# Rests of the down weights from a negated copy and a transfer that adds, in the second gated network of a hybrid decoder trunk

## The chip, the cores and the metric

The kernel runs on one core of a Trainium2 chip. The core has TensorE (PE, matmuls; its weight loads are shown apart as PEld), VectorE (DVE), ScalarE (ACT), GpSimd (POOL) and SyncE (SP), which work side by side and wait for each other by semaphores. 16 DMA engines move data between memory (HBM) and the core's buffer (SBUF); the orders for them stand in queues, here mostly SP's, and for some transfers POOL's. The metric is the device time of one execution in microseconds (us).

## What is computed

Two residual layers over 512 tokens of width 1024: first an S5 mixer, then FoX attention, each followed by a gated network with a causal convolution of width 3. Each part is modulated by shift, scale and gate from a conditioning vector. The part that matters here:

```python
def conv_ffn(h, w_up, conv_w, conv_b, w_down):
    up = h @ w_up
    a, b = jnp.split(up, 2, axis=-1)
    S = a.shape[1]
    ap = jnp.pad(a, ((0, 0), (CONV_W - 1, 0), (0, 0)))
    a_conv = conv_b
    for i in range(CONV_W):
        a_conv = a_conv + ap[:, i:i + S] * conv_w[i]
    return (jax.nn.silu(a_conv) * b) @ w_down

h = h + gate * conv_ffn(hn, ffn_w_up[i], ffn_conv_w[i], ffn_conv_b[i], ffn_w_down[i])
```

Here `w_up` is 1024 x 5632 and `w_down` 2816 x 1024, all in float32, and the tokens lie along the columns of the tiles.

## The kernel before

**Two parts of each number.** A float32 matrix product is done as three matmuls in a rounded format (fp32r): a number is split into its rounded value `hi` and the rest `lo`, and hi·hi + hi·lo + lo·hi is added up in PSUM (`mms`, line 294; in the second way of multiplying below, line 550). A weight tile comes from memory by a load on SP's queue into a buffer `raw` (line 186, three buffers that all weights share in turn), then `put_parts` makes the parts: ACT copies `raw` into `w_hi`, which rounds it (line 277), and DVE subtracts `raw` - `w_hi` into `w_lo` (line 278). Five buffers each of `w_hi` and `w_lo` are shared by these weights in turn. `split` (line 269) is the load and the two parts of one block.

**The gated network** (`ffn`). Its 22 blocks of 128 hidden channels are cut into groups; in the second network these are groups of 6, 5, 6 and 5. The first four blocks use plain products. From then on `quarters` computes both up products of a block (a and b) with seven half-width products in place of eight, which need sums and differences of weights: DVE makes them (line 518, `sums`), ACT and DVE split them, and the products go into two PSUM tiles named `mmp` and two named `aux`. Three of the products are copied out of an `mmp` tile by ACT (`nm_h`, line 557) before PE adds the next product to that tile. A fourth copy is from `aux`. Then follow the convolution and the gate (lines 600, 602, 605 and 612) and the split of the hidden block into `ghi` and `glo` (lines 277 and 278).

**Down products.** While group q is computed, the down products of group q - 1 are worked off: after each hidden block one or two of the eight output tiles (`down` through `product`, `weights` and `split`). One tile takes the down weights of one group for 128 output channels: 6 (or 5) blocks of 128 x 128, so one tile of 128 x 768 (or 640), and 18 (or 15) matmuls of 512 columns (line 294); the third of these is the first that reads `w_lo`. The result is added to the residual by DVE (line 362). The down products of the last group come at the end, behind all blocks.

**What sets the order.** The code names the work of a block in turn; the recording layer then orders the instructions of each engine by when it reckons that each can start. Once built, each engine works its list off in that order, and each waits by semaphores for what it reads and for buffers to come free.

Of the kernel before, what the change touches and what calls it, by code (L numbers as in the profile page):

```python
# [11 lines left out]
AF = mybir.ActivationFunctionType  # L12
ALU = mybir.AluOpType
# [45 lines left out]
def fill(pool, n):  # L59

    pool.tile([P, n // 4], F32, name="fill", bufs=1)
# [5 lines left out]
def part_of(pool, shape, name, tag, bufs, aside=0):  # L67

    _, n, w = shape
    t = pool.tile([P, ROOM if bufs == WB else n * w + P], F32R, name=name, tag=tag, bufs=bufs)  # L70
    return t[:, aside:aside + n * w].rearrange("p (n w) -> p n w", w=w)


class Trunk:
# [6 lines left out]
    def __init__(self, tc, io, ctx):  # L81
        self.tc, self.nc, self.io, self.ctx = tc, tc.nc, io, ctx
        nc = self.nc
        pool = lambda name, bufs, **k: ctx.enter_context(tc.tile_pool(name=name, bufs=bufs, **k))
        self.const = pool("const", 1)
        self.act = pool("act", 1)
        self.wpool = pool("wpool", 3)
        self.tmp = pool("tmp", 2)
        self.small = pool("small", 2)
        self.dram = pool("dram", 1, space=DRAM)  # L90
        self.mm = pool("mm", 4, space=PSUM)
        self.aux = pool("aux", 4, space=PSUM)
        self.bg = []
        self.acc = None
        self.pending = None
        self.normed, self.evac, self.copied, self.squared = [], [], [], []
        self.sums = {}

        self.room = None
        self.one = self.const.tile([P, 1], F32, name="one")  # L100
        nc.vector.memset(self.one, 1.0)
        self.sc = self.const.tile([P, KT], F32, name="sc")
        self.scd = self.dram.tile([KT, P], F32, name="scd")

        self.sel = self.const.tile([P, 6], F32, name="sel")
        nc.gpsimd.memset(self.sel, 0.0)
        for q in range(4):
            for c in (q, 4 + q % 2):
                nc.gpsimd.memset(self.sel[32 * q:32 * q + 1, c:c + 1], 1.0)
        self.par = [self.const.tile([P, 24], F32, name=f"par{i}") for i in range(4)]  # L110
        self.ga = [self.const.tile([P, KT], F32, name=f"ga{i}") for i in range(4)]
        fill(self.const, 1728)
        fill(self.small, 1440 - 1024)
# [155 lines left out]
    def split(self, src, shape, pool=None, bufs=WB, aside=0):  # L269

        hi, lo = (part_of(pool or self.wpool, shape, n, n, bufs, aside) for n in ("w_hi", "w_lo"))
        self.put_parts(hi, lo, self.raw(shape, src))
        return hi, lo

    def put_parts(self, hi, lo, src):
# [307 lines left out]
    def ffn(self, i, l, x, nxt, ticks=0, plain=None):  # L583

        nc, tc = self.nc, self.tc
        with tc.tile_pool(name=f"ffn{l}", bufs=1, reuse_waits="tile") as pool:
            self.bgpool = pool
            conv = pool.tile([P, 4, FT], F32, name="conv_wb")
            nc.sync.dma_start(conv, self.io["conv"][l])
            fill(pool, 1696)  # L590
            cw, cb = conv[:, :3], conv[:, 3]
            groups = QGROUPS[l] if plain else GROUPS
            first = [sum(groups[:q]) for q in range(len(groups) + 1)]
            keep, g = {}, {}

            def gated(m, ps, cols):
                f = m // 2
                if m % 2 == 0:
                    t = pool.tile([P, S], F32, name="conv", bufs=2 if plain else 3)
                    nc.scalar.activation(t, ps, AF.Identity, bias=cb[:, f:f + 1], scale=cw[:, 2, f:f + 1])  # L600
                    for d in (1, 2):
                        c = nc.vector.scalar_tensor_tensor(
                            t[:, d:], ps[:, :S - d], cw[:, 2 - d, f:f + 1], t[:, d:], op0=ALU.mult, op1=ALU.add
                        )
                    nc.scalar.activation(t, t, AF.Silu)
                    keep[f] = t
                    if plain and f >= groups[0]:
                        self.evac = [c.ins]
                        self.tick(ticks)
                    return  # L610
                t = keep.pop(f)
                nc.vector.tensor_tensor(t, t, ps, ALU.mult)
                q = sum(f >= n for n in first[1:])
                j = f - first[q]
                if not j:
                    tag = f"{q % 2}" if plain else ""
                    g[q] = [pool.tile([P, groups[q], S], F32R, name=n, tag=n + tag) for n in ("ghi", "glo")]
                hi, lo = g[q]
                self.put_parts(hi[:, j, :], lo[:, j, :], t)

            after, y = nxt
            up = lambda fs, **k: self.product(
                self.io["w_up"][l], range(2 * fs[0], 2 * fs[-1] + 2), KT, x, gated,
                ticks=0 if plain else ticks, **k
            )
            last = len(groups) - 1
            down = lambda q, ms, **k: self.product(
                self.io["w_down"][l][:, :, first[q]:first[q + 1], :], ms, groups[q], g[q],
                self.add_residual(i, q == last), after=after, ticks=0 if plain else ticks, **k
            )  # L630
            todo = []
            for q, n in enumerate(groups):
                fs = range(first[q], first[q + 1])
                if not plain:
                    up(fs, head=0 if q else 3)
                    if q < last:
                        down(q, range(KT))
                    continue
                for j, f in enumerate(fs):
                    if f == 0:  # L640
                        up([0, 1], head=3)
                        todo.append(self.forms_x(pool, x))
                    elif f in plain:
                        if f > 1:
                            up([f])
                        for _ in range(4):
                            if todo and next(todo[0], True):
                                todo.pop()
                    else:
                        while todo:  # L650
                            if next(todo[0], True):
                                todo.pop()
                        self.quarters(pool, l, f, x, gated)
                    if q:
                        self.room = "rawd" if ticks else None
                        down(q - 1, range(j * KT // n, (j + 1) * KT // n))
                        self.room = None
                        self.tick(ticks)
            down(last, range(KT), tail=TAIL if plain else 2, tail_pool=(pool, 4))
        return y  # L660
# [985 lines left out]
```

## Time and profile before

| | |
|---|---|
| time, median of 3 runs (lowest to highest) | 1214.67 us (1213.35 to 1220.85) |
| profiled execution: its own time | 1217.02 us |
| profiled execution: span from the first to the last instruction | 1215.2 us |
| mean granted clock of PE over the span | 0.995 |
| loads from memory over the span | 175.57 MB read, 6.92 MB written |
| transfers of down weights on SP's queue into `raw`: KB each, us to landing | 384.0, 3.5 and 320.0, 3.1 |

Rows of the profile name the engine, the line of the kernel's file, the operation and `out<-in` by the names of the tiles; `xN` counts instructions. In a row of a group the number behind the bar is the busy time and the mean of one in ns, and behind the second bar stands how long the engine stood idle just before them, and for whom. In a timeline a row begins with the start in us and the duration, and ends with the idle time before it in brackets. In the chain of waits a row is a piece of the chain that ended last: start, length, engine and line. Windows give the busy time of each engine in a stretch.

The second gated network fills about 861 to 1205 us of the span; the part of it from 920 to 1168 us is where the down products of the first three groups are prepared and worked off.

### The profile page before, as it was taken

How to read it: one execution, taken by the hardware profiler on the slowest of the kernel's cores; microseconds unless marked ns; L12 is line 12 of the kernel's file. 1: busy time of each engine (PE TensorE's matmuls, PEld its weight loads, DVE VectorE, ACT ScalarE, POOL GpSimd, SP SyncE). 2: the span in 40 equal slices, each digit the busy share in tenths (PEclk: the TensorE clock that was granted, in tenths of full speed). 3: DMA queues.
4: the chain of work that ended last, by engine and by line, in shares of the span. 5: the costliest groups of instructions: out<-in, count | busy, mean ns of one | idle time of the engine just before them, and what ended most of it. 6: DMA issues, size and time to landing. Idle time of an engine off the chain costs nothing.

```text
span 1215.2 us, 20334 instructions
## 1 busy us (share of the span) xinstructions
PE 1180.3 (97%) x7793; PEld 1015.4 (84%) x7793; DVE 1007.6 (83%) x1872; ACT 609.8 (50%) x1156; POOL 83.9 (7%) x145
## 2 busy tenths in 40 slices
PE   7999999999999999999999999999999999999997
PEld 2566688898989899889899777878989999999987
DVE  7999977789899988898687578875899887888965
ACT  3644555336445454455443565654466554555543
POOL 0000000100000000000000333430000000000000
PEclk9999999999999999999999999999999999999999
DMA  9778786622455544553445543432213332333331
GB/s 348 243 250 261 233 294 220 210 77 70 136 179 164 189 155 148 169 168 106 126 153 180 172 153 130 148 108 88 89 53 113 112 119 90 103 104 109 109 100 70
DMA packets 74512, 183.81 MB, mean 151 GB/s; under 512 B 23231, under 2 KB 25631, under 8 KB 73391
## 3 DMA queue, kind: packets, MB, share of 16 engines
q1 hardware_dynamic: 68367, 161.02, 40.5%
q0 software_dynamic: 5760, 20.97, 5.4%
q8 instruction: 61, 1.00, 0.3%
q10 hardware_dynamic: 288, 0.52, 0.1%
q14 instruction: 36, 0.29, 0.1%
HBM read 175.57 MB, written 6.92 MB: 150 GB/s over the span
## 4 chain that ended last, share of the span: by engine, by line
PE 56%; issue 26%; DVE 8%; DMA 5%; ACT 2%; POOL 2%; SPq 0%; POOLq 0%; DVEq 0%; ACTq 0%
PE mmp L294 24%; PE mmp L550 11%; PE aux L550 4%; PE mmp L1366 3%; PE mmp L1174 2%; DVE w_lo L278 2%; PE mmp L1203 2%; POOL ada_raw L233 1%; PE aux L1505 1%; DMA ada_raw<-in_ada_t 1%; PE aux L1065 1%; PE mmp L1114 1%; PE aux L1057 1%; PE aux L978 1%; DMA yt<-s_yd 1%
## 5 line engine op out<-in xcount | busy, mean ns | idle before, releaser
L278 DVE TENSOR_TENSOR w_lo<-raw,w_hi 128x1024 fp32r<-128x1024 f32 (+4 forms) x173 | 183.3, 1064 | 37.6 <-ACT w_hi L277 31.8
L277 ACT ACTIVATE w_hi<-raw 128x1024 fp32r<-128x1024 f32 (+4 forms) x173 | 154.8, 904 | 105.4 <-PE mmp L294 48.6
L294 PE MATMUL mmp<-ghi,w_hi 128*128 128x512 f32 (+1 forms) x392 | 145.5, 371 | 0.0
L294 PE MATMUL mmp<-ghi,w_lo 128*128 128x512 f32 (+1 forms) x392 | 144.7, 369 | 0.7 <-DVE w_lo L278 0.6
L294 PE MATMUL mmp<-glo,w_hi 128*128 128x512 f32 (+1 forms) x392 | 145.1, 370 | 0.0
L294 PE MATMUL mmp<-a_hi,w_hi 128*128 128x512 f32 (+1 forms) x376 | 138.4, 371 | 1.5 <-ACT a_hi L433 1.5
L294 PE MATMUL mmp<-a_hi,w_lo 128*128 128x512 f32 (+1 forms) x376 | 136.2, 363 | 0.2 <-DVE w_lo L278 0.2
L294 PE MATMUL mmp<-a_lo,w_hi 128*128 128x512 f32 (+1 forms) x376 | 135.7, 362 | 0.0
L550 PE MATMUL mmp<-w_hi 128*128 128x256 f32 x396 | 109.7, 277 | 2.7 <-ACT nm_h L557 2.3
L550 PE MATMUL mmp<-w_hi,w_lo 128*128 128x256 f32 x396 | 109.5, 277 | 0.7 <-DVE w_lo L278 0.7
L550 PE MATMUL mmp<-w_lo,w_hi 128*128 128x256 f32 x396 | 109.4, 276 | 0.0
L557 ACT ACTIVATE nm_h<-mmp 128x256 f32<-128x256 f32 x99 | 37.2, 381 | 107.3 <-PE mmp L550 107.3
L278 DVE TENSOR_TENSOR w_lo<-sums,w_hi 128x1024 fp32r<-128x1024 f32 x74 | 90.0, 1219 | 0.0
L277 ACT ACTIVATE w_hi<-sums 128x1024 fp32r<-128x1024 f32 x74 | 77.0, 1055 | 23.7 <-DVE sums L518 21.7
L294 PEld LDWEIGHTS mmp<-ghi,w_lo 128*128 128x128 f32 x392 | 74.7, 190 | 13.8 <-DVE w_lo L278 1.5
L294 PEld LDWEIGHTS mmp<-ghi,w_hi 128*128 128x128 f32 x392 | 74.7, 191 | 11.5 <-ACT w_hi L277 0.2
L294 PEld LDWEIGHTS mmp<-glo,w_hi 128*128 128x128 f32 x392 | 74.8, 191 | 11.1
L294 PEld LDWEIGHTS mmp<-a_hi,w_hi 128*128 128x128 f32 x376 | 70.2, 188 | 13.8 <-issue 2.6
L294 PEld LDWEIGHTS mmp<-a_hi,w_lo 128*128 128x128 f32 x376 | 70.6, 188 | 12.2 <-DVE w_lo L278 1.2
L294 PEld LDWEIGHTS mmp<-a_lo,w_hi 128*128 128x128 f32 x376 | 70.7, 188 | 9.7
L362 DVE SCALAR_TENSOR_TENSOR h<-mmp,par,h 128x512 f32<-128x512 f32 (+1 forms) x100 | 68.0, 681 | 12.1 <-PE mmp L294 11.9
L550 PEld LDWEIGHTS mmp<-w_hi 128*128 128x128 f32 x396 | 74.3, 188 | 3.2 <-ACT nm_h L557 2.5
(319 smaller groups left out, 3077.7 us busy)
## 6 DMA issues: line engine op xcount, KB each, us to landing
raw<-in_w_up SPq DMA_DIRECT2D x88, 512.0 KB, 3.3
raw<-in_ada_w SPq DMA_DIRECT2D x40, 512.0 KB, 5.6
ada_raw<-in_ada_t POOLq DMA_DIRECT2D x40, 512.0 KB, 3.9
nf<-nfd SPq DMA_DIRECT2D x8, 1152.0 KB, 6.5
raw<-in_fox_qk SPq DMA_DIRECT2D x16, 512.0 KB, 3.7
raw<-in_w_down SPq DMA_DIRECT2D x24, 320.0 KB, 3.1
rawd<-in_w_down SPq DMA_DIRECT2D x24, 256.0 KB, 3.3
raw<-in_w_down SPq DMA_DIRECT2D x16, 384.0 KB, 3.5
```

Of the source, the lines that this page charges most:

```text
L233: (nc.gpsimd if late else nc.sync).dma_start(ws[n], src)
L277: nc.scalar.activation(hi, src, AF.Copy)
L278: return nc.vector.tensor_tensor(lo, src, hi.bitcast(F32), ALU.subtract)
L294: self.last_mm = self.nc.tensor.matmul(o, wt, xt[:, cols], start=(k == 0 and n == 0), stop=(k == nk - 1 and n == 2),)
L362: add = self.nc.vector.scalar_tensor_tensor(self.h[:, m, cols], ps, self.par[i][:, 16 + m:17 + m], self.h[:, m, cols], op0=ALU.mult, op1=A ...
L550: self.last_mm = nc.tensor.matmul(o, wt[:, k], xt[:, k], start=(first and k == 0 and n == 0), stop=(k == H - 1 and n == 2), skip_group_che ...
L557: a = nc.scalar.activation(t, o, AF.Copy)
L978: nc.tensor.matmul(ps[:, :, cols], x[:, q, r].rearrange("p c j -> p (c j)"), both[:, :, planes, q, :], start=(r == 0), stop=(r == 1), skip ...
L1057: nc.tensor.matmul(yp[g2][:, k, :], t[:, g].rearrange("p c i -> p (c i)"), u[:, g, :], start=(k == 0), stop=False, skip_group_check=True,)
L1174: nc.tensor.matmul(ps, w[m][:, k, :], x[:, k], start=(k == 0), stop=(k == KT - 1))
L1203: nc.tensor.matmul(gps[m], wt, xt[:, k], start=(k == 0 and part == 0 and xt is yhi), stop=(k == KT - 1 and part == 1))
L1366: self.last_mm = nc.tensor.matmul(ps[q, b][:, :n], xt[:, k, tb], wt, start=(k == 0 and i == 0), stop=(k == KT - 1 and i == 2),)
```

## The change

In the second gated network, for the down weights of its first three groups, the rest is no longer made by DVE. ACT copies the raw weights twice: into `w_hi`, rounded, and with a factor of -1 into `w_lo`, which then holds the negated rounded value. A transfer on POOL's queue then reads the same raw weights from memory again and adds them to what lies in `w_lo`, so that raw - rounded remains. The down weights of the first network, those of the last group, and all up weights are made as before.

```diff
     def split(self, src, shape, pool=None, bufs=WB, aside=0):
 
         hi, lo = (part_of(pool or self.wpool, shape, n, n, bufs, aside) for n in ("w_hi", "w_lo"))
-        self.put_parts(hi, lo, self.raw(shape, src))
+        raw = self.raw(shape, src)
+        if self.adds:
+            self.nc.scalar.activation(lo, raw, AF.Copy, scale=-1.0)
+            self.nc.scalar.activation(hi, raw, AF.Copy)
+            self.nc.gpsimd.dma_start(lo, src, accum_op=ALU.add)
+        else:
+            self.put_parts(hi, lo, raw)
         return hi, lo
...
                     if q:
                         self.room = "rawd" if ticks else None
+                        self.adds = not ticks
                         down(q - 1, range(j * KT // n, (j + 1) * KT // n))
+                        self.adds = False
                         self.room = None
```

`ticks` is 1 in the first network and 0 in the second; `self.adds` is False from the start.

In the built program PE's list and SP's list hold the same instructions in the same order. The other three move. On ACT, around the first 768-wide down weight of the third group (in the trace of before, the place from 1092 to 1099 us), before:

```order
L277 ACTIVATE w_hi<-raw 128x512
L557 ACTIVATE nm_h<-aux 128x256
L277 ACTIVATE w_hi<-sums 128x1024
L605 ACTIVATE conv<-conv 128x512
L277 ACTIVATE ghi<-conv 128x512
L277 ACTIVATE w_hi<-sums 128x1024
L277 ACTIVATE w_hi<-raw 128x768
L557 ACTIVATE nm_h<-mmp 128x256 x3
```

And now at the same place; the lines of the file are seven higher behind the edit, line 284 is the copy of `put_parts`, 275 and 276 are the two of the new path:

```order
L564 ACTIVATE nm_h<-aux 128x256
L284 ACTIVATE w_hi<-raw 128x512
L284 ACTIVATE w_hi<-sums 128x1024
L612 ACTIVATE conv<-conv 128x512
L276 ACTIVATE w_hi<-raw 128x768
L284 ACTIVATE ghi<-conv 128x512
L275 ACTIVATE w_lo<-raw 128x768
L564 ACTIVATE nm_h<-mmp 128x256 x3
```

The down weight's first copy now stands ahead of the copy of the hidden block and its second copy right behind it; both are still ahead of the three copies out of PSUM.

On DVE, the turn around the same place before, from the sums of a block to its convolution:

```order
L278 TENSOR_TENSOR w_lo<-raw,w_hi 128x768
L518 TENSOR_TENSOR sums<-raw 128x512
L518 TENSOR_TENSOR nm_t<-aux,nm_h 128x256
L518 TENSOR_TENSOR sums<-sums,raw 128x512
L518 TENSOR_TENSOR sums<-raw 128x512
L518 TENSOR_TENSOR sums<-raw,sums 128x512
L278 TENSOR_TENSOR w_lo<-raw,w_hi 128x1024
```

And now:

```order
L525 TENSOR_TENSOR sums<-raw 128x512 x2
L525 TENSOR_TENSOR sums<-sums,raw 128x512
L525 TENSOR_TENSOR sums<-raw,sums 128x512
L525 TENSOR_TENSOR nm_t<-aux,nm_h 128x256
L285 TENSOR_TENSOR w_lo<-raw,w_hi 128x1024
```

The subtraction for the down weight is gone, and the four sums of a block stand in a row ahead of the addition for the output. On POOL's list the 24 transfers stand behind all else that POOL does:

```order
L1505 TENSOR_SCALAR s_8611<-s_8611,sm 128x512 x2
L277 DMA w_lo<-in_w_down 128x768 x8
L277 DMA w_lo<-in_w_down 128x640 x8
L277 DMA w_lo<-in_w_down 128x768 x8
L1647 UNCONDITIONAL_BRANCH
```

Before, the branch followed the row of line 1505 (1496 then) at once.

More of the change, by code (lines that the diff above doesn't have):

```diff
@@ L655, in ffn @@
                         self.room = "rawd" if ticks else None
+                        self.adds = not ticks
                         down(q - 1, range(j * KT // n, (j + 1) * KT // n))
+                        self.adds = False
                         self.room = None
```

## The prediction

> **What bounds the kernel now.** I read the page's table of engines first, then the stage of the second gated network by windows, then the chain of waits there, then the groups of DVE and ACT of that stage, and last single rows around the down weights. The page has TensorE busy for nearly the whole span, and the stage in which the change works (920 to 1168 us, where the down weights of the first three groups are prepared) leaves no gap in it at all.
>
> ```profile
> PE 1180.3 (97%) x7793; PEld 1015.4 (84%) x7793; DVE 1007.6 (83%) x1872; ACT 609.8 (50%) x1156; POOL 83.9 (7%) x145
> 920.00:1168.00 248.00, 248.00 (x1809) 233.11 (x1809) 210.99 (x318) 133.33 (x212) 0.00 (x0) 1.00 0.35 109
> ```
>
> The second line gives, in order, the busy time of PE, its weight loads, DVE, ACT and POOL in the 248 us, the granted clock and the share of the DMA engines. A busy PE need not be a PE at its peak, so I checked its pace in the chain that ended last. One turn of the loop is there from 1095.36 on: seven quarter products of 12 matmuls each, then one down tile of 18.
>
> ```profile
> 1095.36 2.74 PE mmp L550 x24
> 1098.11 1.36 PE aux L550 x12
> 1099.47 2.85 PE mmp L550 x24
> 1102.31 1.36 PE aux L550 x12
> 1103.67 1.36 PE mmp L550 x12
> 1105.03 4.10 PE mmp L294 x18
> ```
>
> The chain is PE after PE with no other engine in it. A 256-column matmul passes every 0.113 us (1.36 / 12) and a 512-column one every 0.228 us (4.10 / 18), and the pieces start where the last one ended. The only irregular piece is the third, 2.85 us for 24 matmuls where the first took 2.74: about 0.1 us. That is all that better preparation of weights could win in this turn; the granted clock is 1.00 already.
>
> **The change part by part.** *What DVE and ACT do.* These are the groups of the two kinds of down weights in the stage; the 640-wide ones are ten here because two belong to the last group, which the change leaves alone.
>
> ```profile
> L278 DVE TENSOR_TENSOR w_lo<-raw,w_hi 128x768 fp32r<-128x768 f32 x16 | 14.9, 949 | 0.6 <-ACT w_hi L277 0.6
> L278 DVE TENSOR_TENSOR w_lo<-raw,w_hi 128x640 fp32r<-128x640 f32 x10 | 8.0, 819 | 0.7 <-ACT w_hi L277 0.7
> L277 ACT ACTIVATE w_hi<-raw 128x768 fp32r<-128x768 f32 x16 | 13.3, 834 | 4.6 <-PE mmp L294 3.5 <-DMA raw<-in_w_down 1.2
> L277 ACT ACTIVATE w_hi<-raw 128x640 fp32r<-128x640 f32 x10 | 7.3, 732 | 3.0 <-PE mmp L294 1.5 <-PE aux L550 0.9 <-PE mmp L550 0.6
> L518 DVE TENSOR_TENSOR sums<-raw 128x512 f32<-128x512 f32 x32 | 21.2, 687 | 23.4 <-DMA raw<-in_w_up 23.4
> ```
>
> DVE loses 16 x 0.949 + 8 x 0.819 = 21.7 us of its 211.0. ACT gains as many copies, 16 x 0.834 + 8 x 0.732 = 19.2 us on 133.3, which makes 152.5 of 248 (61%). Neither is on the chain, so both count nothing toward the end as long as PE finds its weights. DVE's gain goes into its own idle time. The last row shows where it idles: 23.4 us for raw up weights, whose three buffers come free only once DVE has read them. A down weight's buffer is now given back by ACT's second copy and no longer by DVE's late subtraction, so those loads can start sooner; SP issues the same transfers in the same order.
>
> *The new transfer.* 24 transfers are issued on POOL's queue, which has no work in this stage, so nothing but the next transfer stands behind a waiting one. PE waits for the result. No accumulating transfer is in the trace; the nearest rows are the 40 plain loads that POOL issues for the adaLN weights, 512 KB each, in the first gated network.
>
> ```profile
> L233 POOL DMA_DIRECT2D ada_raw<-in_ada_t x40: 527/530/743, 158.4 to 555.2; - x40
> DMA to landing us min/median/max: 3.6/3.9/6.8
> q0 software_dynamic: 5760, 20.97, 5.4%
> ```
>
> Issuing takes 0.53 us, so 24 of them are 12.7 us of an empty queue. From issue to landing it is 3.9 us. The packets took 5.4% of 1215.2 us for 40 loads, 1.64 us each, so 2.26 of the 3.9 us do not depend on size. A down weight has 384 KB (or 320), 1.23 us at that pace. An accumulating transfer must also fetch what lies in the destination. I take twice the bytes, 2.26 + 2.46 = 4.7 us, as an estimate. The low end is the plain price for the smaller size, 3.5 us; the high end is the slowest load seen plus one more such load's packets, 6.8 + 1.64 = 8.4 us. The Trainium skill (Collectives: The Full Stack, section "The bandwidth ceiling: the fold count and why AG ≠ RS ≠ AR") says that a transfer that adds runs at about half the rate of a copy, and that the second source read is the reason, not the addition. No run here shows this yet; by it the landing would also be 4.7 us and the sum the same.
>
> *How much time there is.* For each down weight I take the end of ACT's copy in the trace, add the second copy, and compare with the first matmul that reads the rest, the third of its tile. Two rows show that this one starts 0.3 us after the start of the tile in the chain.
>
> ```profile
> 953.48 8.19 PE mmp L294 x36
> 953.78 0.39 PE L294 MATMUL mmp<-ghi,w_lo 128*128 128x512 f32 x1
> 1105.34 0.39 PE L294 MATMUL mmp<-ghi,w_lo 128*128 128x512 f32 x1
> 946.59 0.83 ACT L277 ACTIVATE w_hi<-raw 128x768 fp32r<-128x768 f32 x1
> 1097.17 1.06 ACT L277 ACTIVATE w_hi<-sums 128x1024 fp32r<-128x1024 f32 x1 [1.89 <-DVE sums L518]
> 1098.14 0.83 ACT L277 ACTIVATE w_hi<-raw 128x768 fp32r<-128x768 f32 x1
> 1098.87 0.64 ACT L557 ACTIVATE nm_h<-mmp 128x256 f32<-128x256 f32 x2
> ```
>
> Copies in a row start 0.73 us apart (1098.14 to 1098.87), so two of them end 0.73 + 0.83 = 1.56 us after the first began. At 1098.14 that is 1099.70, and the rest is read at 1105.34: 5.6 us. At 946.59 it is 948.15 against 953.78: 5.6 us again. These are the two tightest. The next are these, the ACT row first and the tile in the chain behind it:
>
> ```profile
> 1054.33 0.72 ACT L277 ACTIVATE w_hi<-raw 128x640 fp32r<-128x640 f32 x1
> 1062.61 3.42 PE mmp L294 x15
> 930.44 1.36 ACT L277 ACTIVATE w_hi<-raw 128x512 fp32r<-128x512 f32 x2
> 939.83 4.10 PE mmp L294 x18
> 1127.08 0.83 ACT L277 ACTIVATE w_hi<-raw 128x768 fp32r<-128x768 f32 x1
> 1136.41 4.10 PE mmp L294 x18
> 961.79 0.83 ACT L277 ACTIVATE w_hi<-raw 128x768 fp32r<-128x768 f32 x1
> 971.21 4.10 PE mmp L294 x18
> 1077.37 1.25 ACT L277 ACTIVATE w_hi<-raw 128x512 fp32r<-128x512 f32 x2
> 1088.54 6.82 PE mmp L294 x30
> ```
>
> In the same way they leave 7.2, 7.6, 8.1, 8.2 and 9.6 us (a row of "x2" ends with the down weight). One more, the second weight for the tiles from 953.48 on, has 7.4 us, but it lies behind the tight one there, whose wait would cover it. The other 16 have 9.7 us or more. With 4.7 us none is late. With the high end of 8.4 us the waits are 2 x 2.8 + 1.2 + 0.8 + 0.3 + 0.2 = 8.1 us.
>
> *DMA load.* 24 x 2.46 us is 59 us of 248, on top of a share of 0.35, so 0.59. That makes other loads a little later; DVE has the 21.7 us that it was relieved of to take that up.
>
> **Sum.** Removed from the chain: 0.1 us at most. Added: 0, up to 8.1 us at the high end. Against the profiled execution (span 1215.2 us, its own time 1217.02) that is no change. The median of the three runs is 2.35 us below the profiled one, so I count from there: 1214.67 - 0.1, about 1214.5 us.
>
> **The rivals.** *A: the rests land too late.* An addition in the DMA engines might be far slower than two reads; nothing in the trace bounds it. The place is the third matmul of each down tile. With 9 us to landing the waits are 2 x 3.4 + 1.8 + 1.4 + 0.9 + 0.8 = 11.7 us, about 1%: that is the point from which this decides. With 10 us it is 2 x 4.4 + 2.8 + 2.4 + 1.9 + 1.8 + 0.4 = 18.1 us, and a little more from the other 16: 1233 us. For it speaks that the kind is unseen; against it that 9 us would be some 5.5 times the packet time of the plain load, (9 - 2.26) / 1.23.
>
> *B: DVE holds POOL up.* While DVE works without a gap POOL might not get its descriptors written. DVE has runs of 12 us without a gap, from 1088.13 to 1100.36:
>
> ```profile
> 1088.13 0.69 DVE L518 TENSOR_TENSOR sums<-raw 128x512 f32<-128x512 f32 x1 [3.08 <-DMA raw<-in_w_up]
> 1099.41 0.95 DVE L278 TENSOR_TENSOR w_lo<-raw,w_hi 128x768 fp32r<-128x768 f32 x1
> 1101.85 0.69 DVE L518 TENSOR_TENSOR sums<-raw 128x512 f32<-128x512 f32 x1 [1.49 <-DMA raw<-in_w_up]
> 380.00:580.00 200.00, 194.64 (x1296) 176.61 (x1295) 179.25 (x283) 93.38 (x152) 12.17 (x23) 1.00 0.49 158
> ```
>
> Half a run on top of 4.7 us makes 10.7 us, and waits of 2 x 5.1 + 3.5 + 3.1 + 2.6 + 2.5 + 1.1 = 23.0 us: 1238 us. Against it stand the 23 issues of the last row's window, 12.17 us in all, 0.53 us each, beside a DVE that was busy 179.25 of 200 us. The Trainium skill (SBUF — State Buffer, section "🔬 SBUF: two separate sides") warns that a transfer issued from GpSimd sits without descriptors while DVE runs an operation that takes both port pairs; the trace shows none of that in the 40 issues, 0.743 us at the longest.
>
> *C: ACT becomes the bound.* Its copies out of PSUM (nm_h) free the tile that PE adds to next. The row at 1098.87 stands behind a down weight, ends at 1099.5, and the third piece of the chain is the one that is 0.1 us long. If each of the 24 added copies held PE up for its whole 0.7 us, it would be 17 us: 1231 us. Against it: PE returns to such a tile 2.72 us after it was done (two products of 1.36 us), and ACT's copy needs less than 0.4 (0.64 for the two in that row), which leaves some 2.3 us for one or two copies ahead of it; and the 1.89 us that ACT stood before 1097.17 was for DVE, which now has less to do.
>
> *D: faster by over 1%.* That would take 12 us out of a stage whose PE has no gap at full clock; 0.1 us is all I find. 1202 us at best, by a cause that I do not see.
>
> **How the numbers follow.** About 1% is what a measurement of this kernel can tell from no change. The forecast, waits between 0 and 8 us, has 0.81. A, beyond 9 us, has 0.11, since its price is unseen; B 0.02; C with more than 12 us 0.04; D 0.02. So faster 0.02, same 0.81, slower 0.17. The range starts at 1212, a little below the fastest run before (1213.35), holds the high end of the sum (1214.5 + 8.1 = 1222.6) and C's full price (1231), and ends at 1232; outside lie most of A, B and D, some 0.15.
>
> **What would show it.** Right: PE busy for 248 of 248 us in the stage, DVE near 190 us, ACT near 152, and no row in which PE waited for a transfer into w_lo. The time from issue to landing of these transfers decides: near 5 us for the forecast, over 9 us for A; issues far over 0.53 us for B; PE waiting for ACT's nm_h for C. Wrong would be a time over 1227, or PE idle before the third matmul of a down tile.

## The result and the profile after

The changed kernel takes 1222.11 us, median of 19 runs (1216.66 to 1231.98); the kernel before took 1215.49 us in 19 runs beside it (1212.58 to 1220.85). The ratio is 1.0055, with a 95% interval from 1.0036 to 1.0074: about half a per cent slower, small but clear of no change, since with 19 runs each the interval is only 0.2% to either side. The profiled execution took 1221.81 us, its span is 1220.0 us.

First come the page's table of engines and the window of the stage, both of the changed kernel, with the columns of the prediction's first fence:

```profile
PE 1184.2 (97%) x7793; PEld 1017.1 (83%) x7793; DVE 988.0 (81%) x1848; ACT 625.3 (51%) x1180; POOL 103.2 (8%) x169
920.00:1168.00 248.00, 245.35 (x1779) 229.04 (x1778) 189.81 (x291) 147.50 (x233) 20.50 (x24) 1.00 0.52 139
```

DVE lost 21 us in the stage and ACT gained 14 there, with fewer matmuls passed in the same 248 us (1779 for 1809). PE is no longer busy throughout: 2.65 us are missing, at a granted clock of 1.00. What it waited for stands in the view of waits of the changed kernel (who waits, for what: us in all, times, the longest):

```profile
PEld mmp L301 <- DMA w_lo<-in_w_down: 4.4, 4, 2.7
PE mmp L301 <- DMA w_lo<-in_w_down: 2.6, 2, 2.2
```

Before there was no such row. The chain of waits shows what that made of the stage. This is its row at the last of these down tiles in the kernel before (the first is in the prediction):

```profile
1167.78 22.26 PE mmp L294 x100
```

and these are the rows at the first and the last in the changed kernel:

```profile
939.32 1.38 PE mmp L557 x12
940.70 0.03 POOLq L277
...
1172.31 17.70 PE mmp L301 x78
```

A transfer order of POOL's queue now stands in the chain where PE ran on before. From the start of the first down tile to that of the last it was 1167.78 - 939.83 = 227.95 us; it is 1172.31 - 940.70 = 231.61 us now, 3.66 us more. In the timeline of PE the whole of it is found at four tiles, each time at the third matmul (a row is start, duration, what, and in brackets the idle time before it and for whom):

```profile
940.75 0.40 PE L301 MATMUL mmp<-glo,w_hi 128*128 128x512 f32 x1
943.38 0.50 PE L301 MATMUL mmp<-ghi,w_lo 128*128 128x512 f32 x1 [2.24 <-DMA w_lo<-in_w_down]
...
957.66 0.50 PE L301 MATMUL mmp<-ghi,w_lo 128*128 128x512 f32 x1 [0.34 <-DMA w_lo<-in_w_down]
...
1123.00 0.50 PE L301 MATMUL mmp<-ghi,w_lo 128*128 128x512 f32 x1
...
1141.11 0.50 PE L301 MATMUL mmp<-ghi,w_lo 128*128 128x512 f32 x1
```

A 512-column matmul follows the last one after 0.23 us when nothing is in its way. 943.38 comes 2.63 us after 940.75, so 2.40 us late; in the same way the other three are 0.50, 0.13 and 0.25 us late, and the matmul behind each of the four another 0.1. That adds up to 3.7 us.

Last come the transfers, in the groups by tile (min/median/max of the issue in ns) and in the table of DMA of the changed kernel, from 920 us on:

```profile
L277 POOL DMA_DIRECT2D w_lo<-in_w_down x24: 847/855/902, 935.4 to 1166.4; - x24
DMA to landing us min/median/max: 4.9/7.4/9.9
```

```profile
q0 software_dynamic: 3456, 8.91, 20.3%
w_lo<-in_w_down POOLq DMA_DIRECT2D x16, 384.0 KB, 8.0
w_lo<-in_w_down POOLq DMA_DIRECT2D x8, 320.0 KB, 6.4
```

From issue to landing it is 7.4 us in the middle, where the forecast had 4.7, and 8.0 for the wide weights. The packets took 20.3% of the 255 us of this window (920 to 1175) for 24 transfers, 2.16 us each.

### The profile page after: what moved, and what is told of

It reads as the page before. It is cut to its first block, busy times and chain, and to the rows that moved or that the text cites. A ratio compares the mean times of both kernels' runs of the same rounds, so it can differ in the third digit from the quotient of the medians.

```text
span 1220.0 us, 20390 instructions
## 1 busy us (share of the span) xinstructions
PE 1184.2 (97%) x7793; PEld 1017.1 (83%) x7793; DVE 988.0 (81%) x1848; ACT 625.3 (51%) x1180; POOL 103.2 (8%) x169
## 4 chain that ended last, share of the span: by engine, by line
PE 49%; issue 26%; DVE 12%; DMA 8%; ACT 2%; POOL 1%; SPq 0%; POOLq 0%; DVEq 0%; ACTq 0%
PE mmp L301 24%; PE mmp L557 4%; DVE w_lo L285 4%; PE mmp L1375 3%; PE mmp L1183 3%; DMA w_lo<-in_w_down 3%; PE aux L557 2%; PE mmp L1212 2%; DMA rawd<-in_w_down 1%; PE aux L1514 1%; PE aux L1074 1%; PE aux L987 1%; PE mmp L1123 1%; PE aux L1066 1%; DVE ada_raw L248 1%
## 5 line engine op out<-in xcount | busy, mean ns | idle before, releaser
L285 DVE TENSOR_TENSOR w_lo<-raw,w_hi 128x1024 fp32r<-128x1024 f32 (+3 forms) x149 | 161.1, 1084 | 42.8 <-ACT w_hi L284 36.7
L284 ACT ACTIVATE w_hi<-raw 128x1024 fp32r<-128x1024 f32 (+3 forms) x149 | 136.3, 921 | 98.3 <-PE mmp L301 44.8
```

What stands on the lines that cost most here:

```text
L284: nc.scalar.activation(hi, src, AF.Copy)
L285: return nc.vector.tensor_tensor(lo, src, hi.bitcast(F32), ALU.subtract)
```

## The experiments

Three theories were open. Theory 1: the whole loss is PE's wait at a few tiles for rests that land late, and they land late because the transfer adds. Theory 2: the landing is long because each transfer meets loads of SP that ACT's copies have just released. Theory 3: the added copies on ACT, or the added traffic, cost something beside those waits.

### e1_plain: the same transfer without the addition

```diff
-            self.nc.gpsimd.dma_start(lo, src, accum_op=ALU.add)
+            self.nc.gpsimd.dma_start(lo, src)
```

> Leaves out the addition: the transfer on POOL's queue loads the raw weights into w_lo instead of adding them, so the rests are wrong by the rounded value; all else, the places of the 24 transfers and the buffers, is as in the changed kernel. Theory 1 (the loss is PE's wait at a few tiles for rests that take 7.4 us to land, and the addition makes them slow): issue 0.53 instead of 0.855 us, landing near 4 us, no PE wait for w_lo, time within 0.2% of before. Theory 2 (the landing is long because each transfer meets the load that SP issues 0.3 us ahead of it): landing 6 us or more here too, and a wait at the first tile stays. Theory 3 (the loss is the added copies and traffic, not the landing): time as in the changed kernel, ratio 1.004 to 1.007.

Measured: 1215.94 us, ratio 1.0000 (0.9983 to 1.0018). The window and the transfers of this run:

```profile
920.00:1168.00 248.00, 248.00 (x1810) 232.88 (x1809) 192.26 (x294) 150.15 (x238) 12.75 (x24) 1.00 0.44 144
```

```profile
L277 POOL DMA_DIRECT2D w_lo<-in_w_down x24: 527/527/604, 935.6 to 1161.1; - x24
DMA to landing us min/median/max: 3.5/4.5/6.4
```

```profile
q0 software_dynamic: 3456, 8.91, 10.6%
w_lo<-in_w_down POOLq DMA_DIRECT2D x16, 384.0 KB, 4.9
w_lo<-in_w_down POOLq DMA_DIRECT2D x8, 320.0 KB, 4.1
```

PE's gaps are gone, with all copies, all transfers and their order as in the changed kernel. The instruction lists of all five engines are the same in both kernels. So the addition is what makes the rests late. It costs 0.33 us at the issue (0.855 for 0.527), 1.03 us of packets (2.16 for 10.6% x 255 / 24 = 1.13) and 2.9 us to the landing (7.4 for 4.5): more than its packet time explains.

The packet records of the traces show where the rest lies. Four of the 384 KB transfers overlap no other of their queue. In the changed kernel the first packet of these starts 2.4 us after the issue, the packets are spread over 3.8 us, and the landing comes 0.3 us after the last (medians). In e1_plain it is 2.1, 1.5 and 0.3 us. Here the addition lengthens the stretch from the first to the last packet, and hardly the time ahead of it.

### e2_lo_first: the negated copy first on ACT

```diff
-            self.nc.scalar.activation(lo, raw, AF.Copy, scale=-1.0)
-            self.nc.scalar.activation(hi, raw, AF.Copy)
+            neg = self.nc.scalar.activation(lo, raw, AF.Copy, scale=-1.0)
+            with self.behind(neg.ins):
+                self.nc.scalar.activation(hi, raw, AF.Copy)
```

> As the changed kernel, but ACT makes the negated copy first and the rounded one after it, so that the transfer is issued ahead of the raw buffer's release and of the load on SP's queue that follows from it. Theory 1: the transfer starts 0.8 to 2.4 us sooner; the wait of 2.4 us at the first down tile goes and the other three (0.5, 0.13, 0.25 us) too, so the time comes within 0.2% of before. Theory 2 (meeting SP's load): the landing itself also falls by 1 to 2 us. Theory 3 (added copies and traffic): no change from the changed kernel.

Measured: 1231.55 us, ratio 1.0140 (1.0108 to 1.0172), a miss. The forced order did not bring the negated copy forward; it kept its old place among ACT's work and pushed the rounded copy behind it. The waits of this run (the line of `product` is 302 here):

```profile
PEld mmp L302 <- DMA w_lo<-in_w_down: 4.7, 2, 3.6
PE mmp L558 <- ACT nm_h L565: 9.0, 5, 3.0
DVE sums L526 <- DMA raw<-in_w_up: 50.7, 14, 6.3
```

The rests still come late at two tiles, and now PE also waits for ACT's copies out of PSUM, behind a DVE that waits longer for raw loads (50.7 us; 38.0 in the changed kernel, 23.4 before). This is the prediction's rival C, brought about by the experiment, not by the change. As a test of slack it failed. It does say something of theory 2: the transfers land after 6.8 us in the middle, 0.6 less than in the changed kernel, where that theory asked for 1 to 2 less.

### e3_group1: only the 640-wide weights by transfer

```diff
-                        self.adds = not ticks
+                        self.adds = not ticks and q == 2
```

> The transfer only for the second group (eight 640-wide down weights); the first and third groups are made by DVE as before. Theory 1: none of the four tiles that waited is in this group, so no PE wait for w_lo and a ratio to before of 1.000 +- 0.002. Theory 3 (each added copy and transfer costs a little): a third of the loss stays, about 1.002.

Measured: 1217.1 us, ratio 1.0007 (0.9990 to 1.0024). The window, and the landing of the eight transfers that are left:

```profile
920.00:1168.00 248.00, 248.00 (x1803) 232.81 (x1802) 205.11 (x310) 137.98 (x220) 6.87 (x8) 1.00 0.41 118
```

```profile
DMA to landing us min/median/max: 5.1/6.6/7.9
```

The eight transfers add as slowly as in the changed kernel (6.6 against 6.4 us), and cost nothing, since their tiles have the time. What counts is the landing against the slack of the tile, not the landing.

### e4_copy_only: the second copy without the transfer

```diff
             self.nc.scalar.activation(lo, raw, AF.Copy, scale=-1.0)
-            self.nc.scalar.activation(hi, raw, AF.Copy)
-            self.nc.gpsimd.dma_start(lo, src, accum_op=ALU.add)
+            self.put_parts(hi, lo, raw)
```

> As before the change, but with ACT's second copy (negated, into w_lo) ahead of the rounded copy and of DVE's subtraction, which overwrites it; no transfer on POOL's queue. Nothing of the result is left out. Theory 1: no PE wait comes of it, ratio to before 1.000 +- 0.002. Theory 3 in the form that ACT's 19 us of copies delay its copies out of PSUM: PE waits for nm_h and a ratio of 1.004 or more.

Measured: 1217.29 us, ratio 1.0007 (0.9994 to 1.0020); the window of the stage has ACT at 148.89 us and PE at 247.62. What PE lacks there is one wait for a copy out of PSUM:

```profile
1099.62 0.39 PE L556 MATMUL mmp<-w_hi 128*128 128x256 f32 x1 [0.38 <-ACT nm_h L563]
```

So the 24 copies on ACT can hold PE up, but by 0.4 us in this profile and by nothing clear of noise in the medians. As the cause of the loss theory 3 falls for the copies by this run, and for the traffic by e1_plain.

### e6_skip4: four steps (six tiles) made as before

```diff
-                        self.adds = not ticks
+                        self.adds = not ticks and (q, j) not in ((1, 0), (1, 1), (3, 1), (3, 2))
```

> As the changed kernel, but the down weights of four steps (six tiles: the first, second and third of the first group, the second to fourth of the third group), where the trace of the changed kernel has all its waits, are made by DVE as before; 18 of the 24 transfers stay. Theory 1 (all of the loss is these waits): no PE wait for a transfer, ratio to before 1.000 +- 0.002. Theory 3 (each transfer costs something): three quarters of the loss stay, ratio 1.003 to 1.005.

Measured: 1216.42 us, ratio 1.0003 (0.9985 to 1.0021). 18 of the 24 transfers stay, and the loss is gone. In its profile the landing of the 18 is as long as ever, and PE still waits for a rest once, 0.59 us:

```profile
DMA to landing us min/median/max: 5.5/7.6/9.7
```

```profile
999.55 0.50 PE L301 MATMUL mmp<-ghi,w_lo 128*128 128x512 f32 x1 [0.59 <-DMA w_lo<-in_w_down]
```

It also waits once for a copy of ACT out of PSUM (`nm_h`), 0.47 us at 992.62. The loss lies in those few tiles; this is what theory 1 says.

### e8_twice: the rest added twice

```diff
             self.nc.gpsimd.dma_start(lo, src, accum_op=ALU.add)
+            self.nc.gpsimd.dma_start(lo, src, accum_op=ALU.add)
```

> As the changed kernel, but the raw weights are added twice, the second transfer waiting for the first, so that the rests are wrong by the raw value and land at about 15 us. Theory 1 by the slack that each tile has: about half of the tiles wait, 3 to 7 us each, some 50 to 80 us in all, ratio 1.04 to 1.07. If PE's waits were not what costs the time, the ratio would stay under 1.02.

Measured: 1269.79 us, ratio 1.0448 (1.0412 to 1.0484). The same mechanism in large: the second transfer waits for the first, and PE waits for rests at 14 places in the row of its weight loads, over the whole span:

```profile
PEld mmp L302 <- DMA w_lo<-in_w_down: 42.7, 14, 6.8
```

The 42.7 us are the idle time of the weight loads, which is a little longer than what PE loses. In the timeline of PE the third matmul is late at 13 tiles, by 39.0 us in all, and the steps behind them are some 14 us longer than usual, nearly all of it because PE ran at half its pace behind the longest waits; the last section shows that. Together these are about 53 us, and the medians differ by 54.2.

### e5_probe: the transfers by themselves

The kernel before, with 18 transfers in a chain on POOL's queue at the start of the second gated network, each of which waits for the last: plain, plain into a rounded tile, and adding; first of 384 KB, then of 192.

```diff
+        for n in (6, 3):
+            for _ in range(3):
+                nc.gpsimd.dma_start(t[:, :n].bitcast(F32), src[:, :n])
+            for _ in range(3):
+                nc.gpsimd.dma_start(t[:, :n], src[:, :n])
+            for _ in range(3):
+                nc.gpsimd.dma_start(t[:, :n], src[:, :n], accum_op=ALU.add)
```

> The kernel before, with a chain of transfers beside it that nothing uses: at the start of the second gated network POOL issues, each waiting for the one ahead of it, three plain loads of 384 KB as float32, three plain loads of 384 KB into the rounded format, three adding ones of 384 KB, and the same nine with 192 KB. Nothing of the result is left out. If the addition by itself makes the landing long: adding transfers of 384 KB take 6 us or more here too, some 3 us above the plain ones, with 0.85 us to issue. If meeting SP's released load makes it long: about 5 us when few loads are about. If the part that depends on size rules, 192 KB lands 1 us or more sooner than 384 KB when it adds; if a fixed part rules, less than 0.5 us.

Measured: the landings by line in this run, in the order above, from 860 to 907 us (384 KB) and from 907 to 946 us (192 KB):

```profile
L670 POOL DMA_DIRECT2D probe<-in_w_down x3: 536/553/589, 865.5 to 872.9; - x3
DMA to landing us min/median/max: 3.4/3.4/4.9
...
L672 POOL DMA_DIRECT2D probe<-in_w_down x3: 527/527/536, 878.0 to 885.5; - x3
DMA to landing us min/median/max: 3.4/3.5/3.5
...
L674 POOL DMA_DIRECT2D probe<-in_w_down x3: 858/866/897, 889.3 to 902.6; - x3
DMA to landing us min/median/max: 4.9/6.1/6.3
...
L674 POOL DMA_DIRECT2D probe<-in_w_down x3: 856/862/884, 930.7 to 941.1; - x3
DMA to landing us min/median/max: 3.7/4.7/5.1
```

The type costs nothing (3.5 for 3.4 us). The addition costs 2.6 us at 384 KB; at 192 KB an adding transfer takes 4.7 us where the two plain lines had 3.6 and 3.2. So of the 3.1 us that the addition costs in the kernel (8.0 for 4.9), it costs 2.6 in the chain too, and there it costs more for the larger size. The split seen in e1_plain does not hold in the chain: two of the three adding 384 KB transfers start their first packet only 3.2 and 3.5 us after the issue, the plain ones after 1.2 to 1.4.

In the kernel's own place a plain transfer of 384 KB took 4.9 us and an adding one 8.0, that is 1.4 and 1.9 us more than in the chain. That much is left for theory 2; that SP's loads are what makes it was not tried by itself. The traces point to something nearer: most of the 24 transfers come in pairs, for two tiles behind the same hidden block, and overlap. In the first profile of the changed kernel a 384 KB transfer that overlaps no other of its queue lands after 6.8 us, the first of a pair after 7.8, the second after 8.9 (medians of 4, 6 and 6); in e1_plain it is 4.1, 4.7 and 5.7.

### e7_halves: each rest by two transfers

```diff
+            n = shape[1] // 2
-            self.nc.gpsimd.dma_start(lo, src, accum_op=ALU.add)
+            self.nc.gpsimd.dma_start(lo[:, :n], src[:, :n], accum_op=ALU.add)
+            self.nc.gpsimd.dma_start(lo[:, n:], src[:, n:], accum_op=ALU.add)
```

> As the changed kernel, but each rest is added by two transfers, one for the first half of the blocks and one for the second, issued one behind the other. Theory 1 with a landing that grows with size: the first half, which the third matmul of a tile needs, lands at 5 to 6 us, the waits shrink to under 1 us in all, ratio about 1.001. With a landing that is mostly fixed: both halves land at 7 us or more, and the loss stays as in the changed kernel or grows, ratio 1.005 or more.

Measured: 1217.52 us, ratio 1.0013 (0.9997 to 1.0029). The third matmul needs only the first half, and that lands earlier, but only by 0.8 us in the middle (6.6 for 7.4; the first half by its line, the second by its own):

```profile
L278 POOL DMA_DIRECT2D w_lo<-in_w_down x24: 855/855/1166, 933.5 to 1160.9; - x24
DMA to landing us min/median/max: 3.5/6.6/8.9
...
L279 POOL DMA_DIRECT2D w_lo<-in_w_down x24: 1014/1194/1505, 934.1 to 1161.4; - x24
DMA to landing us min/median/max: 4.4/7.4/9.3
```

PE waits at one tile only, the first, 1.28 us. That wins back most of the loss, and still does not beat the kernel before.

### e9_again and e10_again: the changed kernel profiled twice more

The first profile's 3.7 us of waits leave open what makes the 6.6 us between the medians, so the unaltered kernel was profiled again.

> The changed kernel unaltered, profiled once more. The first profile's stage grew by 3.7 us of waits for rests, while the medians differ by 6.6 us. Theory 1 (the whole loss is waits for late rests, and their size varies from execution to execution with the landing): another profile has waits for w_lo of another size, 2 to 12 us in sum from 936 us on, at the same tiles (the first one among them) and possibly at one or two more, and the time from the start of the first down tile to the start of the last one grows over the 227.95 us of before by that sum within 0.3 us. Rival (a fixed cost beside the waits): the waits are again 3.7 us within 0.5 us, and what is missing to 6.6 us lies outside these tiles or in gaps that wait for something else.

> The same kernel a third time, on the same chip: with three profiles the spread of the waits can be seen. Theory 1: the times of the three profiled executions stand in the same order as their sums of waits for rests, and differ by about as much. Rival: they do not follow the waits.

Measured: 1219.30 and 1222.66 us, beside one run of the kernel before at 1212.31. The chain of waits at the first and at the last down tile, of e9_again:

```profile
939.04 0.03 POOLq L277
...
1169.85 28.61 PE mmp L301 x156
```

and of e10_again:

```profile
938.50 0.03 POOLq L277
...
1173.24 26.79 PE mmp L301 x140
```

From the one to the other it is 1169.85 - 939.04 = 230.81 us in e9_again and 1173.24 - 938.50 = 234.74 us in e10_again, 2.86 and 6.79 us more than before. The late steps of PE add up to 3.0 and 6.8 us. The first tile is 0.68 us late in the one, 3.42 in the other, and 2.40 in the first profile; its matmul is due 5.6 us after the issue in all three, and the transfer landed after 6.3, 9.0 and 8.0 us. The second tile is late in all three as well. In the third group the tiles change: the first one of it, on time in the first profile, is late in both of these, in e9_again like this:

```profile
1107.30 0.50 PE L301 MATMUL mmp<-ghi,w_lo 128*128 128x512 f32 x1 [0.45 <-DMA w_lo<-in_w_down]
```

The tile that was late at 1123.00 is late again in e10_again alone (0.07 us), and the one at 1141.11 in neither. Of all 72 transfers of the three profiles, 11 land later after their issue than the matmul is due, and at the third matmul of these 11 tiles, and of no other, PE is late, by that difference within 0.1 us.

So the waits vary from execution to execution because the landing does, and with 2.9, 3.7 and 6.8 us the three times stand in the order of their waits (1219.30, 1221.81, 1222.66). They do not differ by just as much: the first tile starts between 938.50 and 940.70 us, so the stages before differ by up to 2.2 us as well. The three waits have a mean of 4.4 us, which is the low edge of the interval of the difference (0.36% to 0.74%, 4.4 to 9.0 us). For the other 2 us up to the difference of the medians three profiles are too few, and no cause of their own was seen; that the loss as a whole hangs on the late rests is shown by e1_plain and e6_skip4, whose medians are those of before.

## Why the prediction was wrong

The forecast was no change, 1214.5 us; the kernel is 0.55% slower, beyond what the runs are uncertain by, though inside the given range and within 1%. The prediction held that about 1% is what can be told from no change; these runs can tell half of that.

- **The step that failed: the landing of the new transfer.** The prediction took "twice the bytes, 2.26 + 2.46 = 4.7 us". Measured are 7.4 us (8.0 for the wide weights, up to 9.9). The doubled packet time was right in kind and near in size: 2.16 us, 1.9 times the 1.13 us of the plain transfer in e1_plain, where the estimate was 2.46. The Trainium skill (Collectives: The Full Stack, section "The bandwidth ceiling: the fold count and why AG ≠ RS ≠ AR") has a collective that adds (ReduceScatter) run at half the rate of one that copies (AllGather), because the addition reads two sources; the packet times here agree with that. What failed was the 2.26 us beside the packets, taken as fixed: in the changed kernel 7.4 - 2.16 = 5.2 us lie there, and in e1_plain 4.5 - 1.13 = 3.4. About one us of the miss already belongs to the place, where a plain transfer takes 4.5 us and two transfers of the queue overlap for most tiles, which the prediction did not price; the larger part is the addition's, as e1_plain and e5_probe show. By the packet records of the 384 KB transfers that no other overlaps, the time ahead of the first packet and behind the last stayed in the kernel nearly what it is for a plain one; the time between the two is what grew, from 1.5 to 3.8 us, more than the packet time of such a transfer did.
- **The sum at the high end was the right one.** With 8.4 us the prediction had waits of 8.1 us and 1222.6 us; with 8.0 us its table gives 2 x 2.4 + 0.4 = 5.2 us (the 640-wide weight with 7.2 us is in time, since its kind lands after 6.4). The three profiles have 2.9, 3.7 and 6.8. The mechanism was that of rival A, well short of its 9 us. The error lay in taking 4.7 us and not the high end as the forecast for a kind of transfer of which the trace had none.
- **The slack of single tiles was off.** The first tile had 7.6 us in the prediction, from the ACT list of before. On the new list a copy out of PSUM and an activation stand between the two copies, in the timeline of ACT of the changed kernel:

```profile
931.82 0.83 ACT L276 ACTIVATE w_hi<-raw 128x768 fp32r<-128x768 f32 x1
932.62 0.38 ACT L564 ACTIVATE nm_h<-mmp 128x256 f32<-128x256 f32 x1
933.67 0.63 ACT L612 ACTIVATE conv<-conv 128x512 f32<-128x512 f32 x1 [0.67 <-DVE conv L609]
934.21 0.83 ACT L275 ACTIVATE w_lo<-raw 128x768 fp32r<-128x768 f32 x1
```

The second copy ends at 935.04, 3.2 us after the first began and not 1.56; POOL issues at 935.35, 0.3 us later, which the prediction left out, and the matmul was due at 940.98. That leaves 5.6 us from the issue, and 8.0 us to the landing make the 2.4 us of the wait. The tile called tightest, the one from 953.48 on, had 7.0 us in that profile (issue 950.16, due at 957.16, landed after 7.5) and waited 0.5. The other one with 5.6 us had 8.0 (issue 1101.26, matmul at 1109.23, landed after 7.3) and did not wait in that profile; in e9_again and e10_again it had 6.9 and 7.2 and waited. That the table's 5.2 us lies so near the waits measured is in part luck: the first tile had less time than predicted, these two had more. When PE has waited once, all its later tiles are due later, which the prediction's sum of single waits leaves out; whether that is the whole reason was not tried.
- **DVE and ACT.** DVE at 189.8 us in the stage, about 190 as forecast; ACT at 147.5 where 152.5 was forecast (150.15 in e1_plain, where PE runs at full pace). Neither time bounds anything, and e4_copy_only shows the copies to cost nothing clear of noise.
- **DMA share** 0.52, where 0.59 was estimated. That "other loads" get "a little later" was true and larger than thought: DVE waits 38.0 us for raw up weights, 23.4 before, but only 23.7 in e1_plain. DVE had the room.
- **Rival B** did not occur. The issues take 0.855 us and not 0.53, but with a maximum of 0.902 and a plain issue of 0.527 in e1_plain, it is the addition that they pay for; the same issue took 0.86 to 0.90 us in the probe. **Rival C** decided only e2_lo_first; single waits of that kind, of 0.4 and 0.5 us, are in the profiles of e4_copy_only and e6_skip4. **Rival D**, a gain, has nothing in its favour: with the waits for rests gone (e3_group1) or down to one (e6_skip4) the time is that of before, as the PE without gaps said it would be.

## What to carry to other kernels

Where PE had no gap, work taken off another engine won nothing, and a longer path to PE's operands could only lose: so compare the new path's latency with the slack of every tile, first of all the tightest. If the trace has no instance of the new kind of transfer, either time it in a chain of a few beforehand or take the high bound of its landing as the forecast. Read the slack from the issue on the new list, not from the old timeline, since an added step need not land right behind the one that it belongs to, and look which transfers of the new kind will be under way at once.

## What was not expected of the hardware

**A late PE can pay twice.** After long waits PE ran at half pace for some us. In e10_again this followed the 3.42 us at the first tile (timeline of PE):

```profile
942.20 0.50 PE L301 MATMUL mmp<-ghi,w_lo 128*128 128x512 f32 x1 [3.25 <-DMA w_lo<-in_w_down]
...
943.50 0.63 PE L301 MATMUL mmp<-ghi,w_hi 128*128 128x512 f32 x1
943.93 0.63 PE L301 MATMUL mmp<-glo,w_hi 128*128 128x512 f32 x1
```

Steps of 0.43 us in place of 0.23, until 946.1: some eight matmuls, about 1.6 us on top of the wait. The granted clock shows it in the windows behind three waits in e8_twice, of 6.4, 1.9 and 1.9 us:

```profile
943.80:947.90 4.10, 3.90 (x9) 3.13 (x10) 0.00 (x0) 0.99 (x2) 0.00 (x0) 0.50 0.33 96
988.50:992.20 3.70, 3.69 (x9) 2.92 (x10) 2.00 (x3) 1.42 (x3) 0.87 (x1) 0.55 0.48 161
1140.40:1145.00 4.60, 4.56 (x23) 3.89 (x24) 2.56 (x4) 1.99 (x4) 0.85 (x1) 1.00 0.58 151
```

The clock is the third number from the end. It is halved for 4 us behind the long wait; behind the two of 1.9 us it is halved once and full once, and in the first profile of the changed kernel 2.2 us left it full. The Trainium skill (TensorE: Matmul & The Clock Gate, section "🔬 Part 1: The HAM clock gate (the "warmup" mystery)") says that PE's clock falls to half after an idle window of about 3.4 us and needs about 3.4 us of work to come back. The wait of 6.4 us agrees with that. The clock was also halved behind waits of 3.25 us (e10_again) and of 3.2 and 3.0 us (e2_lo_first, granted clock 0.51 and 0.50 in the windows behind them), and once behind 1.9: these are shorter than the page has it.

**An adding transfer's landing grows by more than its packets.** At 384 KB the addition costs 2.6 us in the probe's chain and 3.1 in the kernel, of which the issue has 0.33 and the packets about 1.0. In the kernel most of the remaining time lies between the first and the last packet (see e1_plain), in the chain part of it ahead of the first one; what it is spent on, no view of the trace shows.
